# A two-block transformer kernel on one core: first gate block read early, tile order in the first block, and the last expert tiles by token half

## The chip, the core and the metric

The kernel runs on one core of a Trainium2 chip. The core has a matrix engine (TensorE, PE in the profile), a vector engine (VectorE, DVE), a scalar engine (ScalarE, ACT), GpSimd (POOL) and a queue engine (SyncE, SP) that here issues the transfers between the device memory and the on-chip memory. Matmul results land in eight banks of an accumulation memory (PSUM). The metric is the time of one launch in device microseconds; lower is better.

## The reference, cut to what matters

One sequence of 256 tokens, 1024 wide, all in float32, goes through two models one behind the other. The first is a block with a modulated norm, an input projection to gates, queries, keys and values, a causal convolution over four tokens with silu for the recurrent heads, eight-head causal attention with rotary positions, two output projections that are weighted with sigmoid gates, and a gated feed-forward of width 2816. The second is two layers of mixer, cross attention and an expert layer. The parts that the change touches are these:

```python
z = h @ w_in + b_in                        # mq, mk, mv, mo, mi, mf, aq, ak, av, ga, gb
qk = silu(causal_dwconv([mq, mk], conv_w, conv_b))
merged = sigmoid(ga) * (ym @ p_mlstm) + sigmoid(gb) * (ya @ p_moba)
x = x + g1 * (merged @ w_out)              # g1, sh2, sc2 ... = silu(c) @ ada_w + ada_b
...
# expert layer, per token and head: the 16 best of 128 x 128 key pairs
eid = take_along_axis(cand_id, pos)        # 8 heads x 16 experts of 16384
g = softmax(top)
act = gelu(einsum('td,ted->te', x, u[eid]))
x = x + einsum('te,ted->td', g * act, v[eid])
...
return rms_norm(x, final_norm)
```

## The kernel before

**Dense experts.** The expert layer (`peer`) doesn't gather. It multiplies all 16384 experts: 128 tiles of u (each 128 experts wide, 24 matmuls of 256 tokens, made by `lin_t`), a gelu, a product with a dense matrix of gates, and 128 tiles of v (12 matmuls of 512 columns, `v_tile`). A matmul in full precision is made of three: weights and activations are split into a high and a low part (`split`: a cast on ACT at L335, a difference on DVE at L336), and high x high, high x low and low x high are accumulated.

**Gates.** The dense gate matrix is built in 16 chunks of 16 tokens (L1448): DVE makes one-hot matrices from the expert numbers, PE multiplies them, ACT writes the results into a staging tile `gstg` (L1465), and SP stores the chunk to device memory (`gate_dram`, L1467). Between the steps `fill` runs u tiles. Later `load` (L1475) reads blocks of 8 expert tiles back (`gt`, L1478), one per 8 value tiles, the first when value tile 0 begins. After the chunks four more u tiles run (UX), then value tiles and the remaining u tiles alternate (L1507). The u results of blocks 7 to 9 go to device memory (`act_dram`, L1397) and come back later.

**Value tiles.** `v_tile` multiplies one row of gates with the u result (L1493), splits it and the v weights, and adds into four PSUM banks y, one for each half of the tokens (tb) and of the columns (hf): 12 matmuls at L1500. After tile 127 in layer 0, y is copied (L1525), transposed on PE (L1531), added to x (L1533), squared and scaled chunk by chunk for the next norm. In layer 1 `final` adds y to the transposed x (L1625), squares with a row sum on ACT (L1627), takes the power on POOL, multiplies with the norm's weight row and the row factor in one DVE instruction (L1633) and stores (L1634).

**First block.** Projections of `w_in_t` (37 tiles of 128 columns, `lin_t`) and of `w_in_n` (row-major, `lin_n`, evacuated at L734) are cut into steps. Tiles 0 to 8 and four steps of `w_in_n` run first; the rest is a filler (`both`, L759) that the attention (`moba`) and the recurrence (`mlstm`) call between their own instructions: 8 tiles whose evacuation is the convolution (`conv`, L697 to L702: ACT, three DVE products, ACT, one DVE product), four steps of `w_in_n`, then 4 tiles of `smo` and 16 of `sg`, which ACT evacuates alone (L729, L731). Every third step also runs one step of `ada` (L590): a 1 MB load and two reductions on DVE (L598) that make two columns of modulation. Ten of its twelve steps run there and the last two in the w_out product (L796).

**What sets the order.** Each engine and each queue executes in order. The framework places the instructions on the queues ahead of the run, by the order of the program as priority and by its own times for when operands and buffers are free, so on one queue a later instruction of the program can stand before an earlier one. On-chip buffers come from classes by size (L286): twelve of the largest size, 2064 words a partition, hold u results, gate blocks, staging tiles and split activations; three raw weight buffers of two tiles each and three pairs of split weights serve all weight streams.

## Time and profile before

| | |
|---|---|
| median of three runs | 2528.02 us (2525.88 to 2528.76) |
| the profiled execution's own time | 2529.0 us |
| its span, first to last instruction | 2527.3 us |
| PE busy | 2481.3 us, 98% of the span |
| DVE busy | 1887.2 us, 75% |
| ACT busy | 1293.1 us, 51% |
| POOL busy | 94.5 us, 4% |
| bytes moved | 536.20 MB, mean 212 GB/s |
| mean granted TensorE clock | 0.996 of full |

Busy time is the time in which an engine has at least one instruction under way; PE's matmuls are pipelined, so a busy PE is not PE at its peak. A granted clock of 1.00 is 2.4 GHz, 0.50 is 1.2 GHz.

### The profile page before, as it was taken

The page shows a single profiled execution, that of the slowest core. Times are in us where ns is not written, and L with a number is a line of the kernel's source. Part 1 is how long each engine was busy: PE and PEld are TensorE (multiplying, and loading weights), DVE is VectorE, ACT ScalarE, POOL GpSimd, SP SyncE. Part 2 cuts the span into 40 slices and gives each one's busy share as a digit, 9 for nine tenths or more (in the row PEclk, how much of TensorE's full clock was granted, in tenths as well). Part 3 has the DMA queues.
Part 4 walks back from the last instruction along what each step waited for, and adds up shares of the span by engine and source line. Part 5 has one row for each costly group of instructions (what it writes and reads, how often), then busy time and mean ns, then how long its engine had stood idle before and what let it go on. Part 6 is the DMA issues. An engine that isn't in the chain of part 4 may idle for free.

```text
span 2527.3 us, 44009 instructions
## 1 busy us (share of the span) xinstructions
PE 2481.3 (98%) x17668; PEld 2297.1 (91%) x17668; DVE 1887.2 (75%) x3438; ACT 1293.1 (51%) x2102; POOL 94.5 (4%) x107
## 2 busy tenths in 40 slices
PE   8999999999999999999999999999999999999998
PEld 6879999999999999999888889899999989998887
DVE  7887876686898976555777798767999755556776
ACT  3554555455455555444444563645455544444544
POOL 1000100221000000000000100110000000000000
PEclk9999999999999999999999999999999999999999
DMA  8556565554555796567875544345457866579753
GB/s 336 183 181 229 204 230 205 184 169 150 173 175 199 273 313 221 194 222 241 296 257 193 191 172 150 117 150 167 168 192 270 312 221 212 202 241 298 277 187 130
DMA packets 197468, 536.20 MB, mean 212 GB/s; under 512 B 9232, under 2 KB 82192, under 8 KB 191760
## 3 DMA queue, kind: packets, MB, share of 16 engines
q1 hardware_dynamic: 197264, 533.40, 61.2%
q8 instruction: 138, 2.26, 0.4%
q14 instruction: 66, 0.54, 0.1%
HBM read 492.47 MB, written 40.89 MB: 211 GB/s over the span
## 4 chain that ended last, share of the span: by engine, by line
PE 82%; DVE 8%; issue 6%; DMA 2%; ACT 1%; POOL 0%; SPq 0%; DVEq 0%; POOLq 0%; ACTq 0%
PE mm L1500 23%; PE mm L400 9%; PE mm L401 9%; PE mm L402 9%; PE sm L400 8%; PE sm L401 8%; PE sm L402 8%; DVE wL L336 2%; PE sm L1462 1%; PE sm L1463 1%; PE mm L431 1%; PE mm L432 1%; PE mm L430 1%; DMA gt<-gate_dram 1%; DMA raw<-in_wk 1%
## 5 line engine op out<-in xcount | busy, mean ns | idle before, releaser
L335 ACT CAST wH<-raw 128x1024 fp32r<-128x1024 f32 x789 | 826.6, 1049 | 992.4 <-PE sm L401 312.9
L336 DVE TENSOR_TENSOR wL<-raw,wH 128x1024 fp32r<-128x1024 f32 x789 | 966.8, 1226 | 455.4 <-ACT wH L335 449.8
L400 PE MATMUL sm<-uH,wH 128*128 128x256 f32 x2048 | 584.3, 285 | 2.1 <-ACT wH L335 2.0
L402 PE MATMUL sm<-uH,wL 128*128 128x256 f32 x2048 | 577.3, 282 | 3.8 <-DVE wL L336 3.8
L401 PE MATMUL sm<-uL,wH 128*128 128x256 f32 x2048 | 578.6, 283 | 0.0
L400 PE MATMUL mm<-nH,wH 128*128 128x256 f32 (+1 forms) x1432 | 410.6, 288 | 4.6 <-ACT qraw L726 2.4
L401 PE MATMUL mm<-nL,wH 128*128 128x256 f32 (+1 forms) x1432 | 404.8, 283 | 1.2 <-DVE nL L616 1.0
L402 PE MATMUL mm<-nH,wL 128*128 128x256 f32 (+1 forms) x1432 | 403.6, 283 | 0.8 <-DVE wL L336 0.6
L400 PEld LDWEIGHTS sm<-uH,wH 128*128 128x128 f32 x2048 | 386.3, 189 | 6.6 <-ACT wH L335 2.5
L402 PEld LDWEIGHTS sm<-uH,wL 128*128 128x128 f32 x2048 | 386.0, 189 | 5.6 <-DVE wL L336 5.6
L401 PEld LDWEIGHTS sm<-uL,wH 128*128 128x128 f32 x2048 | 386.7, 189 | 3.6
L1500 PE MATMUL mm<-wH,pwh 128*128 128x512 f32 x1024 | 317.6, 391 | 4.0 <-ACT pwh L335 4.0
L1500 PE MATMUL mm<-wL,pwh 128*128 128x512 f32 x1024 | 316.8, 391 | 0.0
L1500 PE MATMUL mm<-wH,pwl 128*128 128x512 f32 x1024 | 316.3, 390 | 0.0
L400 PEld LDWEIGHTS mm<-nH,wH 128*128 128x128 f32 x1432 | 270.1, 189 | 9.8 <-issue 3.5
L401 PEld LDWEIGHTS mm<-nL,wH 128*128 128x128 f32 x1432 | 270.9, 189 | 2.1 <-DVE nL L616 1.2
L402 PEld LDWEIGHTS mm<-nH,wL 128*128 128x128 f32 x1432 | 270.2, 189 | 2.5 <-DVE wL L336 1.4
L1500 PEld LDWEIGHTS mm<-wL,pwh 128*128 128x128 f32 x1024 | 192.8, 188 | 41.2
L1500 PEld LDWEIGHTS mm<-wH,pwl 128*128 128x128 f32 x1024 | 192.5, 188 | 41.0
L1500 PEld LDWEIGHTS mm<-wH,pwh 128*128 128x128 f32 x1024 | 185.8, 188 | 37.3 <-ACT pwh L335 4.4
L1493 DVE TENSOR_TENSOR pw<-act,gt 128x256 f32<-128x256 f32 x256 | 108.6, 424 | 19.9 <-DMA gt<-gate_dram 12.6
L336 DVE TENSOR_TENSOR pwl<-pw,pwh 128x256 fp32r<-128x256 f32 x256 | 108.8, 425 | 12.6 <-ACT pwh L335 6.6
(452 smaller groups left out, 3085.6 us busy)
## 6 DMA issues: line engine op xcount, KB each, us to landing
raw<-in_u SPq DMA_DIRECT2D x128, 1024.0 KB, 5.0
raw<-in_v SPq DMA_DIRECT2D x128, 1024.0 KB, 5.0
gate_dram<-gstg SPq DMA_DIRECT2D x32, 1024.0 KB, 4.8
gt<-gate_dram SPq DMA_DIRECT2D x32, 1024.0 KB, 8.3
raw<-in_ada SPq DMA_DIRECT2D x24, 1024.0 KB, 4.9
raw<-in_w_gu SPq DMA_DIRECT2D x22, 1024.0 KB, 4.9
raw<-in_w_in_t SPq DMA_DIRECT2D x18, 1024.0 KB, 5.1
raw<-in_pq SPq DMA_DIRECT2D x16, 1024.0 KB, 5.0
```

The source lines that it names most:

```text
L335: self.nc.scalar.copy(H, src)
L336: self.nc.vector.tensor_sub(L, src, H.bitcast(F32))
L400: mm(ps[:, :w], H[:, o:o + P], xH[:, c], start=c == 0, stop=False)
L401: mm(ps[:, :w], H[:, o:o + P], xL[:, c], start=False, stop=False)
L402: mm(ps[:, :w], L[:, o:o + P], xH[:, c], start=False, stop=c == kc - 1)
L430: mm(pss[tb], xh, H[:, o:o + 512], start=c == 0, stop=False)
L431: mm(pss[tb], xl, H[:, o:o + 512], start=False, stop=False)
L432: mm(pss[tb], xh, L[:, o:o + 512], start=False, stop=c == kc - 1)
L1462: nc.tensor.matmul(ps[:, k * P:k * P + P], at(ah), at(o1), start=True, stop=False)
L1463: nc.tensor.matmul(ps[:, k * P:k * P + P], at(al), at(o1), start=False, stop=True)
L1493: nc.vector.tensor_mul(w.rearrange("p (c t) -> p c t", c=16), act[b][:, j].rearrange("p (c t) -> p c t", c=16), box[b][:, :, j])
L1500: nc.tensor.matmul(y[tb * 2 + hf], a[:, sl], m[:, hf * 512:hf * 512 + 512], start=n == 0 and a is wh and m is vH, stop=n == P - 1 and a is wl)
```

## The change

It has five parts. The weight columns of `w_in_t` are reordered so that the eight convolution tiles and the first eight gate tiles alternate, and the filler takes sixteen tiles before it turns to `w_in_n`; the evacuation follows the new numbering. The last two steps of `ada` run after tile 3 of p_moba and tile 3 of w_out, in place of tiles 2 and 5 of w_out. In the expert layer the first gate block gets its tile `gfirst` before the chunks; chunks 0 to 13 are loaded into it from device memory after chunk 13 is stored, and the parts of chunks 14 and 15 are copied by ACT out of the staging tile. The matmuls of the last three value tiles are held back and made at tile 127, token half 0 first, then token half 1 by column half; the copies behind them in layer 0 follow that order. In `final`, x is multiplied with the norm's weight row ahead of the power, and the product with the row factor is made by ACT for one column half and by DVE for the other.

```diff
 RB = 7
 SB = 3
-VL, RI, MD, UX, M1, M2, D1, D2, AS, AW, PQ0, NQ0, FT, F0, FH, FS, FL, FO = 6, 5, 1, 4, 1.25, 1.5, 0.5, 0.75, 3, 3, 13, 3, 0.6, 1, 0.5, 1, 4, 1.075
+VL, RI, MD, UX, M1, M2, D1, D2, AS, PQ0, NQ0, FT, F0, FH, FS, FL, FO = 6, 5, 1, 4, 1.25, 1.5, 0.5, 0.75, 3, 13, 3, 0.6, 1, 0.5, 1, 4, 1.075
 REPL = -3e38
 GSCALE = 16384.0
...
     A["positions"] = np.ascontiguousarray(i["positions"])
     A["final_row"] = np.ascontiguousarray(i["final_norm_2"].reshape(1, D))
     A["ada"] = _pack_rows(i["ada_w"][0])
-    A["w_in_t"] = _pack_t(np.concatenate([gate, w_in[:, 2056:3080], w_in[:, 0:1024], w_in[:, 1536:2048], w_in[:, 3592:5640]], axis=1))
+    A["w_in_t"] = _pack_t(np.concatenate([gate, w_in[:, 2056:3080], *(w for j in range(8) for w in (w_in[:, j * P:j * P + P], w_in[:, 3592 + j * P:3720 + j * P])), w_in[:, 1536:2048], w_in[:, 4616:5640]], axis=1))
     A["w_in_n"] = _pack_n(np.concatenate([w_in[:, 3080:3592], w_in[:, 1024:1536]], axis=1))
     A["b_nat"] = np.ascontiguousarray(np.concatenate([b_in[3080:3592], b_in[1024:1536]])[None])
     A["p_mlstm"] = _pack_t(i["p_mlstm"][0])
...
                 turn.append((e - 1, raw))
                 if e > 1:
                     rope(*turn.pop(0))
-            elif e < 17:
+            elif e < 25 and e % 2:
+                c = (e - 9) // 2
                 raw = self.t(None, "qraw", [P, T])
-                nc.scalar.activation(raw, ps, AF.Identity, bias=self.vec("b_qk", e - 9))
-                conv(e - 9, raw)
-            elif e < 21:
-                nc.scalar.activation(smo[:, e - 17], ps, AF.Tanh, scale=0.5, bias=hb[:, e - 17:e - 16])
+                nc.scalar.activation(raw, ps, AF.Identity, bias=self.vec("b_qk", c))
+                conv(c, raw)
+            elif 24 < e < 29:
+                nc.scalar.activation(smo[:, e - 25], ps, AF.Tanh, scale=0.5, bias=hb[:, e - 25:e - 24])
             else:
-                nc.scalar.activation(sg[:, e - 21], ps, AF.Tanh, scale=0.5, bias=hb[:, e - 17:e - 16])
+                c = (e - 10) // 2 if e < 25 else e - 21
+                nc.scalar.activation(sg[:, c], ps, AF.Tanh, scale=0.5, bias=hb[:, 4 + c:5 + c])
         def evac_n(g, tb, ps):
             nc.vector.tensor_add(vnat[:, g, tb], ps, b_nat[:, g * 512:g * 512 + 512])
...
         next(mg)
         def rest():
-            for _ in range(8):
+            for _ in range(16):
                 yield next(zt)
             yield from zn
             yield from zt
...
             nc.vector.tensor_add(m, a, merged[:, e])
             self.split(mH[:, e], mL[:, e], m)
+        moved = []
         for g in (self.lin_t("p_moba", 8, 4, (ya[:, :4], ya[:, 4:]), ev_ma), self.lin_t("p_mlstm", 8, 4, (ym[:, :4], ym[:, 4:]), ev_mm)):
-            self.run(g)
+            for i, _ in enumerate(g):
+                if i == 3 and not moved:
+                    moved.append(next(ada, None))
         nc.vector.tensor_scalar(self.mod[:, 16:24], self.mod[:, 16:24], 0.5, None, op0=ALU.mult)
         geff = self.t(None, "geff", [P, 8])
         nc.vector.scalar_tensor_tensor(out=geff, in0=self.mod[:, 32:40], scalar=1.0, in1=self.vecn("norm2", 0, 8), op0=ALU.add, op1=ALU.mult)
         n2 = Norm(self, geff)
         n2.shift = self.mod[:, 24:32]
         for i, _ in enumerate(self.lin_t("w_out", 8, 8, (mH, mL), self.residual(n2, lambda e: self.mod[:, 16 + e:17 + e]))):
-            if i % AW == AW - 1:
+            if i == 3:
                 next(ada, None)
         self.run(ada)
         self.tap("xa", self.x)
...
             nc.vector.tensor_scalar(ghlT[:, sl, 0], gT, GSCALE, None, op0=ALU.mult)
             nc.vector.scalar_tensor_tensor(out=ghlT[:, sl, 1], in0=gT, scalar=GSCALE, in1=ghlT[:, sl, 0], op0=ALU.mult, op1=ALU.subtract)
         gd = self.dram.tile([16, P, P * 16], F32, name=f"gate_dram{l}")
+        gfirst = self.t(None, "gt", [P, 16, P])
         for ch in range(16):
             stg = self.t(None, "gstg", [P, P, 16])
             for sub in range(2):
...
                     nc.scalar.activation(dst, ps.rearrange("p (t i) -> p i t", t=4), AF.Copy, scale=1.0 / GSCALE)
                 self.fill(FO)
             nc.sync.dma_start(gd[ch], stg.rearrange("p i t -> p (i t)"))
+            i0 = 8 * order[0]
+            if ch == 13:
+                nc.sync.dma_start(gfirst[:, :14], gd[:14, :, i0 * 16:i0 * 16 + P].rearrange("c p f -> p c f"))
+            elif ch > 13:
+                nc.scalar.copy(gfirst[:, ch], stg[:, i0:i0 + 8].rearrange("p i t -> p (i t)"))
         self.drain()
         for _ in range(UX):
             next(u_gen)
...
         def load(n):
             b = order[n]
-            gt = self.t(None, "gt", [P, 16, P])
-            nc.sync.dma_start(gt, gd[:, :, b * P:b * P + P].rearrange("c p f -> p c f"))
+            gt = self.t(None, "gt", [P, 16, P]) if n else gfirst
+            if n:
+                nc.sync.dma_start(gt, gd[:, :, b * P:b * P + P].rearrange("c p f -> p c f"))
             box[b] = gt.rearrange("p c (i t) -> p c i t", i=8)
             if RB <= b < RB + SB:
                 act[b] = self.t(None, "act", [P, 8, T])
                 nc.sync.dma_start(act[b].rearrange("p i t -> p (i t)"), sd[b - RB])
+        rest = []
         def v_tile(n):
             if n == 0:
...
             nc.vector.tensor_mul(w.rearrange("p (c t) -> p c t", c=16), act[b][:, j].rearrange("p (c t) -> p c t", c=16), box[b][:, :, j])
             self.split(wh, wl, w)
             vH, vL = next(vst)
-            for tb in range(2):
-                sl = slice(tb * P, tb * P + P)
-                for a, m in ((wh, vH), (wh, vL), (wl, vH)):
-                    for hf in range(2):
-                        nc.tensor.matmul(y[tb * 2 + hf], a[:, sl], m[:, hf * 512:hf * 512 + 512], start=n == 0 and a is wh and m is vH, stop=n == P - 1 and a is wl)
+            rest.append([(hf, a, m, n == 0 and a is wh and m is vH, n == P - 1 and a is wl) for a, m in ((wh, vH), (wh, vL), (wl, vH)) for hf in range(2)])
+            if n < P - 3:
+                products(0)
+                products(1)
+                rest.clear()
+            elif n == P - 1:
+                products(0)
+                for p in rest:
+                    p.sort(key=lambda q: q[0])
+                products(1)
+        def products(tb):
+            for hf, a, m, first, last in chain(*rest):
+                nc.tensor.matmul(y[tb * 2 + hf], a[:, tb * P:tb * P + P], m[:, hf * 512:hf * 512 + 512], start=first, stop=last)
         if l == 1:
...
         out = Norm(self, self.vecn("mix_norm", 8, 8))
         out.late = out.fast = True
         ys = []
-        for g in range(2):
-            for tb in range(2):
+        for tb in range(2):
+            for g in range(2):
                 yt = self.t(None, "py", [P, 512])
-                (nc.scalar.copy if tb else nc.vector.tensor_copy)(yt, y[tb * 2 + g])
+                (nc.scalar.copy if g else nc.vector.tensor_copy)(yt, y[tb * 2 + g])
                 ys.append(yt)
         for g in range(2):
             for tb in range(2):
                 ps = self.sm()
                 for c in range(4):
-                    nc.tensor.transpose(ps[:, c * P:c * P + P], ys[g * 2 + tb][:, c * P:c * P + P], self.ident)
+                    nc.tensor.transpose(ps[:, c * P:c * P + P], ys[tb * 2 + g][:, c * P:c * P + P], self.ident)
                 xs = self.x[:, 4 * g:4 * g + 4, tb * P:tb * P + P]
                 nc.vector.tensor_add(xs, xs, ps.rearrange("p (c t) -> p c t", c=4))
             for c in range(4):
...
                 nc.vector.tensor_add(xs, xs, y[tb * 2 + hf])
                 junk = self.t(None, "fj", [P, 512])
                 nc.scalar.activation(junk, xs, AF.Square, accum_out=ss[:, hf:hf + 1])
+            xf = [self.t(None, "fx", [P, 512]) for _ in range(2)]
+            for hf in range(2):
+                nc.vector.tensor_mul(xf[hf], xn[:, tb, hf * 512:hf * 512 + 512], frow[:, hf * 512:hf * 512 + 512])
             nc.vector.tensor_add(ss[:, :1], ss[:, :1], ss[:, 1:])
             r = self.pow_col(ss[:, :1], 1.0 / D, EPS, 1)
             for hf in range(2):
                 sl = slice(hf * 512, hf * 512 + 512)
                 o = self.t(None, "fo", [P, 512])
-                nc.vector.scalar_tensor_tensor(out=o, in0=xn[:, tb, sl], scalar=r, in1=frow[:, sl], op0=ALU.mult, op1=ALU.mult)
+                if hf:
+                    nc.vector.tensor_scalar(o, xf[hf], r, None, op0=ALU.mult)
+                else:
+                    nc.scalar.activation(o, xf[hf], AF.Copy, scale=r)
                 nc.sync.dma_start(self.out[0, tb * P:tb * P + P, sl], o)
     def build(self):
```

## Rows read from the trace of the kernel before

**Rows 1.** The page, its first part: busy us, share of span, instructions.

```profile
PE 2481.3 (98%) x17668; PEld 2297.1 (91%) x17668; DVE 1887.2 (75%) x3438; ACT 1293.1 (51%) x2102; POOL 94.5 (4%) x107
```

**Rows 2.** Windows: stretch, length, then each engine's busy us; clock, DMA share, GB/s.

```profile
118.00:200.00 82.00, 76.29 (x488) 63.40 (x487) 73.21 (x192) 46.29 (x103) 4.98 (x8) 0.96 0.50 180
146.00:156.00 10.00, 9.85 (x29) 6.47 (x30) 7.12 (x18) 5.17 (x13) 1.41 (x2) 0.66 0.18 74
250.00:300.00 50.00, 47.93 (x398) 47.20 (x397) 46.86 (x82) 25.59 (x42) 6.13 (x6) 1.00 0.62 214
```

**Rows 3.** Timeline of PE, the stage with the convolution: start, length, idle before.

```profile
141.59 0.39 PE L400 MATMUL mm<-nH,wH 128*128 128x256 f32 x1 [2.38 <-ACT qraw L726]
```

**Rows 4.** Single lines of code on DVE: shortest, median and longest ns.

```profile
L699 DVE SCALAR_TENSOR_TENSOR qk<-qraw,vecs,qk x24: 347/476/676, 126.0 to 173.9; 128x255 f32<-128x255 f32 x8, 128x254 f32<-128x254 f32 x8, 128x253 f32<-128x253 f32 x8
L702 DVE SCALAR_TENSOR_TENSOR qk<-ra,qk x8: 405/426/685, 131.1 to 175.0; 128x256 f32<-128x256 f32 x8
L598 DVE CUSTOM_DVE_ANT_0 adaj<-raw,cb x48: 1199/1218/1753, 21.5 to 379.5; 128x1024 bf16<-128x1024 f32 x48
```

**Rows 5.** Timeline of SP's queue around the first layer's last gate chunks.

```profile
916.45 1.03 SPq L1467 DMA_DIRECT2D gate_dram<-gstg  x1
...
931.83 0.33 SPq L1467 DMA_DIRECT2D gate_dram<-gstg  x1
...
938.49 0.37 SPq L1478 DMA_DIRECT2D gt<-gate_dram  x1
940.56 3.35 SPq L1397 DMA_DIRECT2D act_dram<-sact  x2
```

**Rows 6.** Timeline of PE before the first value matmul, both expert layers.

```profile
946.11 0.39 PE L400 MATMUL sm<-uH,wH 128*128 128x256 f32 x1 [1.02 <-ACT wH L335]
...
947.96 0.72 PE L1500 MATMUL mm<-wH,pwh 128*128 128x512 f32 x2 [1.35 <-ACT pwh L335]
...
2028.16 0.39 PE L400 MATMUL sm<-uH,wH 128*128 128x256 f32 x1 [1.02 <-ACT wH L335]
...
2031.32 1.02 PE L1500 MATMUL mm<-wH,pwh 128*128 128x512 f32 x2 [2.65 <-ACT pwh L335]
```

**Rows 7.** Windows: last gate chunks of layer 0, first value tiles of layer 1.

```profile
900.00:941.00 41.00, 41.00 (x406) 40.67 (x404) 28.96 (x25) 23.56 (x40) 0.00 (x0) 1.00 0.92 319
2031.00:2035.00 4.00, 3.68 (x9) 2.91 (x10) 3.06 (x7) 1.35 (x4) 0.00 (x0) 0.57 0.67 198
```

**Rows 8.** An ACT copy of 128x128, shortest, median and longest ns.

```profile
L504 ACT COPY pT<-sm x16: 254/272/307, 128.2 to 1620.4; 128x128 f32<-128x128 f32 x16
```

**Rows 9.** Timeline of PE behind the value tiles of layer 0.

```profile
1436.21 0.62 PE L400 MATMUL mm<-nH,wH 128*128 128x256 f32 x3 [0.91 <-ACT nH L236]
```

**Rows 10.** Chain of waits, value matmuls before the end: start, us, count.

```profile
2298.87 198.59 PE mm L1500 x876
```

**Rows 11.** Timeline of the last microseconds.

```profile
2510.40 1.23 DVE L336 TENSOR_TENSOR wL<-raw,wH 128x1024 fp32r<-128x1024 f32 x1 [1.49 <-ACT wH L335]
...
2517.75 0.61 PE L1500 MATMUL mm<-wH,pwl 128*128 128x512 f32 x2
...
2518.25 1.28 DVE L1625 TENSOR_TENSOR xn<-xn,mm 128x512 f32<-128x512 f32 x2 [0.16 <-ACT fj L1627]
...
2520.12 0.18 ACT L1627 ACTIVATION_READ_ACCUMULATOR fj<-xn 128x1 f32 x1
...
2521.78 0.15 DVE L1628 TENSOR_TENSOR fss<-fss 128x1 f32<-128x1 f32 x1
...
2522.80 1.41 DVE L1633 SCALAR_TENSOR_TENSOR fo<-xn,pr,frow 128x512 f32<-128x512 f32 x2 [0.67 <-POOL pr L473]
```

**Rows 12.** Store of the output: KB, us to landing; 128x512 copies of ACT.

```profile
out<-fo SPq DMA_DIRECT2D x4, 256.0 KB, 2.0
...
L1525 ACT COPY py<-mm x2: 586/589/592, 1432.9 to 1433.3; 128x512 f32<-128x512 f32 x2
```

**Rows 13.** Timeline of ACT, first staging writes of layer 0's last chunk.

```profile
926.92 1.08 ACT L1465 ACTIVATE gstg<-sm 128x512 f32<-128x512 f32 x2
```

## The prediction, made before the result was known

> **What bounds the kernel now.** I read the page's engine table first: TensorE (PE) is busy for 98% of the span, VectorE (DVE) for 75% [rows 1]. So the kernel is a long PE stream, and a change that removes no matmul can only win back PE idle time (2527.3 - 2481.3 = 46.0 us), half-clock time, and the tail behind the last matmul. I then cut the span into stages at the places that the diff touches.
>
> Stage one is the part of the first block in which projections, convolution and block attention run together, 118 to 200 us. In its 82 us PE is busy 76.3, so idle 5.7, while DVE is busy 73.2; around 146 to 156 us the granted clock averages 0.66 [rows 2]. With levels of 1.0 and 0.5 that is 10 x (1 - 0.66) / 0.5 = 6.8 us at half clock, which costs 3.4 us of matmul work. The longest single gap, 2.38 us, ends on ACT's copy of a convolution tile out of PSUM (L726) [rows 3]: the evacuation was late, not the weights. What the gaps and the slow clock hold together is 5.7 + 3.4 = 9.1 us.
>
> Stage two is the p_moba, p_mlstm and w_out products, 250 to 300 us: PE idle 2.1 us, DVE busy 46.9 of 50 [rows 2].
>
> Stage three is the hand-over from building the gates to the value products, once in each expert layer. The store of the last gate chunk is issued at 931.83 and the load of the first gate block only at 938.49, when that store has landed (6.7 us); PE runs out of work twice before the first value matmul at 947.96 [rows 5, 6]. The gaps are 1.02 + 1.35 = 2.4 us in layer 0 and 1.02 + 2.65 = 3.7 us in layer 1 [rows 6]. In layer 0 the clock stayed at full level; in layer 1 it averages 0.57 over the 4 us that follow [rows 7], 3.4 us at half clock, 1.7 us lost. Together 2.4 + 3.7 + 1.7 = 7.8 us.
>
> The last is the two ends of the expert layers. At the end of layer 0 PE waits 0.91 us for the first normalized chunk [rows 9]. At the very end the last matmuls finish at 2517.75 + 0.61 = 2518.36 [rows 11], so 8.9 us of the span lie behind them.
>
> **First block: order of the tiles.** Matmuls, evacuations and vector instructions stay as many; 8 gate tiles now stand between the 8 convolution tiles. One convolution costs DVE three products of 0.48 and one of 0.43, 1.86 us, eight of them 14.9 us [rows 4]. Before, they come in eight successive filler steps; now they are spread over sixteen, and the two groups of row-major products (L734 evacuates them) come behind them. The upper bound is all of the 9.1 us, the lower bound nothing, since DVE's work is the same. DVE gives the estimate: it is busy 73.2 of 82 us, so the stage can't shrink by more than 8.8 even with DVE at 100%. I take half of 9.1: **4.5 us**.
>
> **First block: modulation rows.** The last two of the twelve steps (each two reductions of 1.22 us on DVE [rows 4] and a 1 MB load) move from tiles 2 and 5 of w_out to tile 3 of p_moba and tile 3 of w_out. Nothing is removed, so at best the 2.1 us of idle PE go; at worst the 2.4 us of reductions make p_moba's weight splits late instead. DVE has only 3.1 us free in these 50, so I take less than half: **0.9 us**. The extra load passes SP ahead of p_mlstm's and w_out's weights; I cost that at nothing, as DVE is the full engine there and the weights stand in SP ahead of their use, and keep the loss of 2.4 as bound.
>
> **Gate hand-over.** The load of chunks 0 to 13 can go when chunk 13's store has landed: 916.45 + 6.7 = 923.1 on the old clock. It then needs some 8.5 us (from the issue at 938.49 to the first matmul at 947.96 is 9.5, of which the product and the cast take about one), so it is there at about 931.6, when chunk 15 is just being stored. Chunks 14 and 15 come by two copies on ACT of 128x128, 0.27 us each [rows 8], four in both layers, 1.1 us; they hide behind matmuls, since PE is busy for all of 900 to 941 us while ACT is busy 23.6 of 41 [rows 7]; uncovered they would cost that 1.1 us. PE comes free at 946.11 - 1.02 = 945.1 [rows 6], some 12 us after the operands. What remains are transitions; I take **7.0 us** of the 7.8, between bounds of 0 (below) and 7.8.
>
> **Last expert tiles by token half.** The 36 matmuls of the last three tiles stay. A matmul of this shape takes 198.59 / 876 = 0.227 us of the stream [rows 10], so token half 0 is now complete 18 x 0.227 = 4.1 us before the end, and the first column half of token half 1 2.0 us before it. PE now needs tile 127's operands early: it starts the 36 at about 2518.4 - 36 x 0.227 = 2510.2 (some 0.3 sooner with the four transposes that stood between them) and comes to tile 127 after 12, at about 2512.6. The last of that tile's weight splits was done at 2510.40 + 1.23 = 2511.6 [rows 11]. So no stall is my value; the margin of 1 us is thin, and 1.4 us (half 0 of a tile late by its own length) goes into the bound below. In layer 0 three of four copies out of PSUM now lie under matmuls; the additions and squares behind the transposes stay on the path. Of the 0.9 us gap there I take **0.5**, bounds 0 and 0.9.
>
> In layer 1 I rebuild the tail. Before: DVE's two additions for token half 1 end at 2518.25 + 1.28 = 2519.53, ACT has squared and summed at 2520.12 + 0.18 = 2520.30, but DVE joins the two sums only at 2521.78, because the output products of half 0 keep it busy; half 1's products run from 2522.80 to 2524.2, and the last store lands 2.0 after that [rows 11, 12]. Now half 0 is out of the way. After the last matmul: 0.1 and one addition, 0.64; ACT's square to the end of its accumulator, 2520.30 - 2519.53 = 0.8; joining, scaling and power to the start of the product, 2522.80 - 2521.78 = 1.0; one product, 0.71; a second store issue behind the first, 0.4 (SP's issues take 0.33 to 0.37 [rows 5]); landing 2.0; the 1.1 us that the span runs on (2527.3 - 2526.2). That is 6.8 against 8.9: **2.1 us**. The half of the product that goes to ACT costs no more than its 128x512 copies, 0.59 [rows 12]; the four added products with the norm row, 0.71 each on DVE like the products they precede, run while ACT squares; if none of that cover held it would cost 1.4. Bounds -0.7 (that, and the 1.4 above) and 3 (the four additions of half 0 and their squares are wholly gone from the tail).
>
> The Trainium skill ("VectorE: DVE Perf Modes", section "The perf-mode tier table") lets a tensor-by-scalar product in fp32 from SBUF run twice as fast as a product of two tensors. By it the last product on DVE would be about 0.3 us shorter and the sum 0.3 us larger; no row here has this shape, and the sum above doesn't use it.
>
> **Sum.** 4.5 + 0.9 + 7.0 + 0.5 + 2.1 = 15.0 us off the profiled execution's 2529.0, 2514.0. That execution is 1.0 above the median 2528.02, so against the median I forecast **2513**.
>
> **Rivals.**
> *One: the alternation gives nothing.* For it: DVE, not PE, is the fullest engine of stage one for long stretches, and no DVE instruction goes. Against it: the 2.38 us gap sits on a convolution evacuation. Time: 2513 + 4.5 = 2517.5.
> *Two: the hand-over still waits.* SP waits for chunk 13's store before it can issue the load; if the load stands directly behind that store, SP is held 6.3 us, and weight loads behind it are late while the DMA engines are already 92% busy [rows 7]. The wait on the gate block becomes one on weights. Against it: before, the load was issued just as the store landed, and two activation stores that the program has ahead of it were issued after it, from 940.56 [rows 5]; the order of SP is planned by time, not by program. Time: 2513 + 7.0 = 2520. The Trainium skill ("DMA: Bandwidth & Descriptors", "Anatomy of one DMA — SWDGE (gpsimd) path") says that a semaphore wait happens on the issuing sequencer, before dispatch; this speaks for this rival, and the trace agrees only so far that SP is in order.
> *One and two together:* 2524.5, within the bound of no change.
> *Three: slower, by buffers.* The early gate tile takes one of the 12 slots of its size. Two slots hold the split activations and seven the u results, so three were left for staging, two now. A chunk's first write to staging comes 4.9 us before its store (926.92 to 931.83) and stores come 7.7 apart [rows 5, 13]: with two slots it comes 15.4 - 4.9 = 10.5 us after the store that frees the slot, which lands in 6.7; no wait. Should another tile of that size be alive and only one slot be left, it comes 7.7 - 4.9 = 2.8 after, and each chunk is 6.7 - 2.8 = 3.9 us late. For some 12 chunks a layer that is 94 us: about 2607. It decides from five late chunks on (20 us against the 15). Against it: the count above.
>
> **How the numbers follow.** What counts as a change for this kernel is 0.2%, 5 us. Forecast 0.52 (its own range 2508 to 2517, from the halves that I took); rival one 0.20; two 0.12; both 0.09; three 0.07. Leaving out three and both together (0.16) and a few hundredths at the low end, where every term is near its bound (9.1 + 2.1 + 7.8 + 0.9 + 3 = 22.9 would be 2505), the range is 2506 to 2523. Faster: 0.52 + 0.20 + 0.12 less 0.05 for cases one and two that end above 2523, 0.79; same 0.09 + 0.05 = 0.14; slower 0.07.
>
> **What would show it.** In the profile after: no gap before the first value matmul in either layer and no half clock behind it (hand-over right); the load of the first gate block issued about 15 us before the first value matmul; the gap on L726's convolution copy gone and PE idle below 3 us between 118 and 200 (alternation right); DVE idle near zero there with the stage still 82 us long (rival one); PE waiting for a weight split between chunks 13 and 15 (rival two); ACT's staging writes waiting for stores, chunks over 8 us apart (rival three); last matmul to end of span 6.8 us. A wrong count of what DVE can still take in stage one would make the forecast wrong soonest.

## The result, and the profile after

The changed kernel takes 2512.63 us in the median of five runs (2510.81 to 2513.2), against 2528.02 before: ratio 0.9937, 95% interval 0.9926 to 0.9947. Its profiled execution took 2513.2 us with a span of 2511.5, 15.8 less than before. The forecast was 2513. All times here are medians of fast runs; one of the twelve runs of undo_handover below, 2682.23 us, was slow and is left out.

The engine table of the page, against [rows 1]: PE has lost 6.7 us of busy time (part of it half-clock time) and 9.1 of idle.

```profile
PE 2474.6 (99%) x17668; PEld 2293.0 (91%) x17668; DVE 1885.4 (75%) x3440; ACT 1294.5 (52%) x2108; POOL 97.8 (4%) x107
```

Where the 15.8 lie, from instructions that both timelines have, as the change of each distance (times in the span before and after in brackets): up to the first weight gap of the first block (71.93 before, 72.93 after) +1.0, within the start's own variation (71.1 to 73.0 in all runs); to the end of the recurrence (244.39, 240.88) -4.5; to the row sums behind w_out (299.30, 294.54) -1.25; to layer 0's gates (781.30, 776.71) +0.2; to the last value matmul of layer 0 (1433.04, 1426.63) -1.8; to the first mixer matmul (1436.21, 1430.09) +0.3; to layer 1's gates (1861.11, 1854.07) -0.9, in stages that the change doesn't touch; to the last value matmul (2518.36, 2504.37) -6.95; to the end of the span -1.8.

The windows of the changed kernel answer to [rows 2]; columns as there.

```profile
118.00:200.00 82.00, 80.10 (x524) 68.17 (x524) 74.25 (x195) 46.99 (x107) 8.35 (x8) 0.96 0.54 191
154.00:158.00 4.00, 2.71 (x14) 2.15 (x15) 3.90 (x15) 3.01 (x9) 0.00 (x0) 0.81 0.68 258
158.00:162.00 4.00, 4.00 (x14) 2.70 (x14) 4.00 (x6) 0.47 (x2) 2.81 (x2) 0.50 0.42 108
162.00:166.00 4.00, 4.00 (x31) 4.00 (x31) 2.91 (x7) 1.58 (x3) 0.00 (x0) 0.84 0.78 258
250.00:300.00 50.00, 48.94 (x409) 48.21 (x408) 44.67 (x75) 26.49 (x42) 7.00 (x7) 1.00 0.63 212
```

Stage one has 1.9 us of PE idle left of 5.7, and the gap of [rows 3] is gone. But the stretch at 0.50 (1.2 of 2.4 GHz) is not: (0.19 + 0.50 + 0.16) x 4 / 0.5 = 6.8 us, as long as before, now behind two short gaps:

```profile
154.66 0.38 PE L400 MATMUL mm<-nH,wH 128*128 128x256 f32 x1 [0.81 <-ACT wH L335]
...
156.12 0.43 PE L512 MATMUL sm<-pT,vnat 128*64 128x128 f32 x2 [0.63 <-ACT pT L504]
...
918.79 0.22 PE L1469 MATMUL sm<-oo,oa 128*128 128x128 f16 x1 [0.82 <-ACT sact L1401]
...
940.16 0.72 PE L1525 MATMUL mm<-wH,pwh 128*128 128x512 f32 x2
```

The last row is the first value matmul, with no gap in front, against [rows 6]; layer 1 has none either and keeps full clock. The row above it is new: a gap of 0.82 among the last gate chunks, one in each layer. The timelines of ACT and SP show what is late there. Chunk 14's staging writes come at 918.64, all four at once, 7.7 behind chunk 13's second pair, where chunk 13's two pairs are 3.8 apart:

```profile
907.13 1.08 ACT L1472 ACTIVATE gstg<-sm 128x512 f32<-128x512 f32 x2
910.95 1.08 ACT L1472 ACTIVATE gstg<-sm 128x512 f32<-128x512 f32 x2
918.64 2.05 ACT L1472 ACTIVATE gstg<-sm 128x512 f32<-128x512 f32 x4
920.72 0.30 ACT L1479 COPY gt<-gstg 128x128 f32<-128x128 f32 x1
```

```profile
912.05 0.80 SPq L1474 DMA_DIRECT2D gate_dram<-gstg  x1
...
918.54 0.37 SPq L1477 DMA_DIRECT2D gt<-gate_dram  x1
...
920.72 1.21 SPq L1474 DMA_DIRECT2D gate_dram<-gstg  x1
...
928.51 0.32 SPq L1474 DMA_DIRECT2D gate_dram<-gstg  x1
```

The early load goes out 6.5 us behind chunk 13's store and 21.6 ahead of the first value matmul. At the end of layer 0, against [rows 9], the gap in front of the mixer has grown to 1.64: a weight split now stands between the copies out of PSUM and the additions. The first rows are DVE's before the change, where the last split starts 1.6 us ahead of the end of the value matmuls (1433.04). The rows after the change follow; there it starts 0.15 behind that end (1426.63).

```profile
1431.45 1.23 DVE L336 TENSOR_TENSOR wL<-raw,wH 128x1024 fp32r<-128x1024 f32 x1 [1.50 <-ACT wH L335]
1432.60 1.28 DVE L1525 COPY py<-mm 128x512 f32<-128x512 f32 x2
```

```profile
1426.17 0.68 DVE L1550 COPY py<-mm 128x512 f32<-128x512 f32 x1
...
1426.78 1.21 DVE L336 TENSOR_TENSOR wL<-raw,wH 128x1024 fp32r<-128x1024 f32 x1
...
1427.91 2.47 DVE L1558 TENSOR_TENSOR x_res<-x_res,sm 128x512 f32<-128x512 f32 x4
...
1430.09 0.62 PE L400 MATMUL mm<-nH,wH 128*128 128x256 f32 x3 [1.64 <-ACT nH L236]
```

The tail, against [rows 11], is 2511.5 - 2504.37 = 7.13 us. Both sums are there at 2505.96, but the join starts at 2506.31, behind the two products with the norm row:

```profile
2503.91 1.28 DVE L1650 TENSOR_TENSOR xn<-xn,mm 128x512 f32<-128x512 f32 x2
...
2505.10 1.28 DVE L1655 TENSOR_TENSOR fx<-xn,frow 128x512 f32<-128x512 f32 x2
...
2505.77 0.19 ACT L1652 ACTIVATION_READ_ACCUMULATOR fj<-xn 128x1 f32 x1
2506.31 0.15 DVE L1656 TENSOR_TENSOR fss<-fss 128x1 f32<-128x1 f32 x1
...
2507.31 0.72 ACT L1664 ACTIVATE fo<-fx,pr 128x512 f32<-128x512 f32 x1 [1.35 <-POOL pr L473]
2507.31 0.49 DVE L1662 TENSOR_SCALAR fo<-fx,pr 128x512 f32<-128x512 f32 x1 [0.67 <-POOL pr L473]
```

The product by one scalar takes 0.49 here, a product of two tensors 0.64. The Trainium skill ("VectorE: DVE Perf Modes", "The perf-mode tier table") gives the first twice the rate, for operands of 2048 elements; the trace, with 512, agrees in the direction, not in the size.

### The profile page after: what moved, and what is told of

Read it like the earlier page. It is cut to its first block, busy times and chain, and to the rows that moved or that the text cites. A ratio compares the mean times of both kernels' runs of the same rounds, so it can differ in the third digit from the quotient of the medians.

```text
span 2511.5 us, 44019 instructions
## 1 busy us (share of the span) xinstructions
PE 2474.6 (99%) x17668; PEld 2293.0 (91%) x17668; DVE 1885.4 (75%) x3440; ACT 1294.5 (52%) x2108; POOL 97.8 (4%) x107
## 3 DMA queue, kind: packets, MB, share of 16 engines
q8 instruction: 138, 2.26, 0.4%
## 4 chain that ended last, share of the span: by engine, by line
PE 84%; DVE 7%; issue 6%; DMA 1%; ACT 1%; POOL 0%; SPq 0%; POOLq 0%; DVEq 0%; ACTq 0%
PE mm L1525 23%; PE mm L400 9%; PE mm L402 9%; PE mm L401 9%; PE sm L400 8%; PE sm L401 8%; PE sm L402 8%; DVE wL L336 2%; PE sm L1469 1%; PE sm L1470 1%; PE mm L432 1%; DMA raw<-in_ada 1%; PE mm L430 1%; PE mm L431 1%; PE sm L1011 1%
```

## The experiments

All are edits of the changed kernel, timed against the kernel before on the same chip. They were timed in three sessions, in which the kernel before took 2528.2, 2529.8 and 2528.9 us, so 1 or 2 us between two kernels of different sessions say little by themselves; there the distances in the traces decide. "Stage one" below is the distance from the first block-attention matmul (125.14 in the changed kernel) to the end of the recurrence (240.88): 115.7 after, 120.2 before.

**The order of the first block's tiles, undone** (undo_tile_order).

```
-            elif e < 25 and e % 2:
+            elif e < 17:
...
-            for _ in range(16):
+            for _ in range(8):
```

> The changed kernel with only the order of the first block's tiles put back (eight convolution tiles in a row). Theory: the alternation is worth the 4.5 us by which the shift of the first block's landmarks grew over that stage in the changed kernel (from +1.0 at 72 us to -3.5 at the end of the recurrence), all of it from shorter gaps, since the half-clock stretch only moved (6.8 us at half clock before and after). Time 2517.1 (2512.6 + 4.5); the 2.4 us gap before L400 that ends on the convolution's copy returns near 141 us, and PE idle in 118 to 200 us is about 5.7 again instead of 1.9. Rival (the alternation gives nothing, and the first block is shorter through the moved modulation steps or by chance): 2512.6 to 2514, idle in 118 to 200 stays near 1.9.

Measured: 2513.92, ratio 0.9944 (0.9931 to 0.9957), 1.3 above the changed kernel and not to be told from it. The gap is back, PE idle is 82 - 77.3 = 4.7, and stage one takes 117.5:

```profile
140.95 0.38 PE L400 MATMUL mm<-nH,wH 128*128 128x256 f32 x1 [2.34 <-ACT qraw L726]
```

So neither theory holds as written. The gaps are the alternation's, as the first says; the time follows only in part, for two reasons that lie in the clock. The half-clock stretch of stage one is 3.4 us here and 6.8 in the changed kernel. It differs between kernels whose first block is the same: 3.4 us in undo_handover, 10.2 in gate_tile_in_quarters; with one profiled execution of each, whether the kernel or the execution decides is open. And at the end of layer 0, which the edit doesn't touch, the clock falls to half for 3.4 us behind a gap as long as the changed kernel's, and the mixer's first part takes 1.4 us longer (9.5 instead of 8.1). PE's timeline and windows of this run, then the same window of the changed kernel:

```profile
1430.61 0.62 PE L400 MATMUL mm<-nH,wH 128*128 128x256 f32 x3 [1.65 <-ACT nH L236]
1430.00:1436.00 6.00, 5.26 (x29) 5.06 (x30) 6.00 (x17) 5.51 (x16) 0.00 (x0) 0.72 0.63 257
1430.00:1436.00 6.00, 5.79 (x47) 5.59 (x47) 5.90 (x16) 5.00 (x15) 0.00 (x0) 1.00 0.58 236
```

What the alternation takes away in stage one is best read where the stretches are equally long: 2.6 us with 3.4 at half clock (117.5 here, 114.9 in undo_handover) and 4.5 us with 6.8 (120.2 before, 115.7 after). Without the cost of the stretch, taken as half its length, stage one takes 115.8 here and 116.8 before in the old order, and 111.9 to 113.2 in nine kernels with the new.

**The gate hand-over, undone** (undo_handover).

```
-            if ch == 13:
-                nc.sync.dma_start(gfirst[:, :14], ...)
-            elif ch > 13:
-                nc.scalar.copy(gfirst[:, ch], ...)
...
-            gt = self.t(None, "gt", [P, 16, P]) if n else gfirst
+            gt = self.t(None, "gt", [P, 16, P])
```

> The changed kernel with the gate block of the first eight value tiles loaded after the last chunk again, no early tile and no copies. Theory: the hand-over is worth what the landmarks moved across it, 1.8 us in layer 0 and 6.9 us in layer 1, 8.7 in all, which is already net of a new 0.82 us gap per layer in front of chunk 14: time 2521.3; gaps before the first value matmul of 1.0 + 1.4 us in layer 0 and 1.0 + 2.7 us in layer 1, with a half-clock stretch of some 3.4 us behind the second; both 0.82 us gaps gone. Rival (part of layer 1's 6.9 us belongs to a clock stretch that comes and goes by itself, or to drift elsewhere): 2517 to 2519, layer 1's gap back but no half clock behind it.

Measured: 2523.2 in the median of eleven runs (2517.7 to 2526.8), ratio 0.998 (0.9972 to 0.9989), so some 10.6 slower, more than the theory. Between the landmarks layer 0 loses 2.9 and layer 1 7.8. The gaps come back, and at both the clock falls (PE's timeline, then windows):

```profile
940.43 1.22 PE L1518 MATMUL mm<-wH,pwh 128*128 128x512 f32 x2 [1.65 <-ACT pwh L335]
2026.09 1.22 PE L1518 MATMUL mm<-wH,pwh 128*128 128x512 f32 x2 [2.26 <-ACT pwh L335]
2024.00:2034.00 10.00, 7.91 (x22) 6.27 (x23) 5.06 (x10) 2.85 (x6) 0.00 (x0) 0.66 0.96 304
940.00:946.00 6.00, 5.57 (x18) 4.51 (x19) 3.34 (x8) 2.63 (x6) 0.00 (x0) 0.72 0.79 301
```

That is 6.8 and 3.4 us at half clock, where the kernel before had 3.4 and none. Gaps of 1.02 + 1.65 and 1.02 + 2.26, and 5.1 for the clock, make 11.0; the two gaps of 0.82 that are gone give some 2.5 back (next run). Some 2 us are left, and the trace shows two things outside that sum: at the end of layer 0 the clock is at half for 3.4 us, as in undo_tile_order, some 1.5 us; and in layer 1 five groups of eight value tiles take 44.80 us each instead of 44.53, 1.35 together. Why this pace differs is open: it is 44.80 in the kernel before too, and 44.37 in undo_tile_order, which has the hand-over of the changed kernel.

**The new gap of 0.82** (gate_tile_in_quarters, thirteen_slots).

```
-        gfirst = self.t(None, "gt", [P, 16, P])
+        gfirst = [self.t(None, "gt4", [P, 4, P]) for _ in range(4)]
...
-            if ch == 13:
-                nc.sync.dma_start(gfirst[:, :14], ...)
+            for k, c0, c1 in {5: [(0, 0, 4)], 9: [(1, 4, 8)], 13: [(2, 8, 12), (3, 12, 14)]}.get(ch, ()):
+                nc.sync.dma_start(gfirst[k][:, :c1 - c0], gd[c0:c1, ...])
```

> The changed kernel with the early gate tile held in four tiles of a smaller buffer class (four chunks each), so that it takes no slot of the staging tiles' ring; three of the four loads go out earlier, and the product of the first eight value tiles is cut in four. Theory (the early gate tile holds up chunk 14's staging tile through the ring of buffers): the 0.82 us gap near 918.8 and 1997.9 us goes in both layers, chunk 14 is stored 7.7 us behind chunk 13 instead of 8.7; 24 more products on DVE per layer hide. Time 2512.6 - 1.6 = 2511.0. Rival (the gap comes from SP's queue being held by the wait for chunk 13's store, whatever the tile): the gap stays or moves to other chunks, 2512.6 or more.

Measured: 2508.59, ratio 0.9919 (0.9906 to 0.9932), 4.0 below the changed kernel. Both gaps are gone and chunk 14 is stored 7.7 behind chunk 13, although SP holds the load as long as before (6.4 us behind the store; its queue):

```profile
911.48 0.32 SPq L1474 DMA_DIRECT2D gate_dram<-gstg  x1
917.90 0.37 SPq L1477 DMA_DIRECT2D gt<-gate_dram  x1
919.18 0.33 SPq L1474 DMA_DIRECT2D gate_dram<-gstg  x1
```

So SP's wait is not the cause. The gain is 4.0 and not 1.6: from the gates to the first value matmul each layer is 1.25 shorter, and layer 1's groups of eight tiles take 44.4 us, five of them some 0.8 us less together. That second part need not be the edit's, since undo_tile_order has it with the old gate tile. The edit does three things at once (another class, earlier and smaller loads, a product in four parts), and no run takes them apart.

```
-    CLASSES = ((32, 14), (128, 8), (256, 14), (512, 8), (1024, 4), (2064, 12))
+    CLASSES = ((32, 13), (128, 8), (256, 14), (512, 4), (1024, 4), (2064, 13))
```

> The changed kernel with thirteen buffers of the largest class instead of twelve (four of the 512-element class given up for it), the early gate tile as changed. It asks why chunk 14's staging writes come late in the changed kernel (at 918.64, right behind the issue of the early load at 918.54, instead of 7.7 us behind chunk 13's at 914.8). Theory one (slots: two staging slots are too few): with a thirteenth slot chunk 14 is on time and the 0.82 us gap goes. Theory two (order: buffers of one class are handed out in the order of the program, so chunk 14's tile gets its slot only when the early gate tile ahead of it has had its first write, which is the load that waits for chunk 13's store): the gap of 0.82 stays in both layers, though a slot is free. One look; time as the changed kernel, or a few us more where the smaller class runs short.

Measured: 2528.75 in a single run. Some 16 us are lost elsewhere, far more than foreseen (8 us in layer 0's value tiles, 8.8 in layer 1's); that the smaller classes cost them (one buffer of the smallest went too) is not shown. The gap of 0.83 stays in both layers. ACT's timeline:

```profile
909.19 1.08 ACT L1472 ACTIVATE gstg<-sm 128x512 f32<-128x512 f32 x2
912.73 0.38 ACT L1401 ACTIVATE sact<-sm 128x256 f32<-128x256 f32 x1
916.54 0.38 ACT L1401 ACTIVATE sact<-sm 128x256 f32<-128x256 f32 x1
916.82 2.05 ACT L1472 ACTIVATE gstg<-sm 128x512 f32<-128x512 f32 x4
```

The load went out at 917.07, behind these writes, so in this run they did not wait for it: they stand late in ACT's order itself, behind the activation at 916.54. A further slot doesn't help, the quarters in another class do; that speaks for theory two, the order in which the program is laid out around the shared ring. That the planner does it this way is inferred from the two kernels, not seen.

**The token halves and the last product** (three runs).

```
-            if n < P - 3:
+            if n < P - 3 or l == 0:
```

> The changed kernel with the last three value tiles of layer 0 in their old order (each tile's matmuls together) and the old order of the copies there; layer 1 as changed. Theory (in layer 0 the token-half order loses 0.3 us, because the mixer's first weight splits now stand between the copies and the additions): from the last value matmul of layer 0 to the first matmul of the mixer 3.1 to 3.2 us instead of 3.46, gap in front of it 0.9 instead of 1.64; time 2512.3, which is too little for the clock on the wall to tell. Rival (the order is worth 0.5 us in layer 0, as the forecast had it, and something else took 0.8): the distance grows to 3.9 or more, time 2513.1.

Measured: 2512.82, ratio 0.9935 (0.9922 to 0.9948), no difference in time to the changed kernel. In the timeline the distance is 1429.82 - 1426.65 = 3.17 and the gap 0.92; the theory holds, the order loses 0.3 in layer 0. It can lose more: of the seven kernels with the long gap (1.62 to 1.65) in front of the mixer two show the half-clock stretch behind it that costs some 1.5 us, of the seven with the short one (0.91 to 0.92) none. For both layers undone the line is `if n < P:`.

> The changed kernel with the last three value tiles of both layers in their old order, the last product split over ACT and DVE as changed. Theory: undoing the split of the product alone took the tail from 7.13 to 7.78 us, so of the 1.8 us that the tail won the token-half order has the other 1.2: tail 8.3, layer 0's end 0.27 shorter; time 2512.6 + 1.2 - 0.3 = 2513.5. Rival (with the old order the four norm-row products stand among four additions behind the last matmul, 4 x 0.64): tail 9.0 or more, as long as before the change; time 2514.2 or more. Rival (the token-half order is nothing by itself): tail 7.1.

Measured: 2516.36, ratio 0.995 (0.9938 to 0.9962), 3.7 above the changed kernel. The tail is 2514.4 - 2504.09 = 10.3 us, longer than before the change: the rival's size. Half 0's norm-row products now run ahead of half 1's second addition, and half 1's own come after it, all four behind the last matmul:

```profile
2504.57 1.29 DVE L1654 TENSOR_TENSOR fx<-xn,frow 128x512 f32<-128x512 f32 x2
...
2505.84 0.68 DVE L1649 TENSOR_TENSOR xn<-xn,mm 128x512 f32<-128x512 f32 x1
...
2507.65 1.29 DVE L1654 TENSOR_TENSOR fx<-xn,frow 128x512 f32<-128x512 f32 x2
```

```
-                if hf:
-                    nc.vector.tensor_scalar(o, xf[hf], r, None, op0=ALU.mult)
-                else:
-                    nc.scalar.activation(o, xf[hf], AF.Copy, scale=r)
+                nc.vector.scalar_tensor_tensor(out=o, in0=xn[:, tb, sl], scalar=r, in1=frow[:, sl], ...)
```

> The changed kernel with only the last product of the output put back: both halves on DVE as one product of three operands, no products with the norm row ahead of it. Theory: in the changed kernel the two norm-row products of 0.64 each stand between the last addition and the join of the two sums and hold it up by 0.35 us (the accumulators end at 2505.96, the join starts at 2506.31), while the split of the last product over ACT and DVE saves one product of 0.71 in a row: undone, the tail is 0.35 us longer, 7.5 instead of 7.13, time 2513.0. The join then starts within 0.1 us of the second accumulator. Rival (the split of the product was worth the whole gain of the tail): 8.5 or more. Rival (the late join eats it all): 7.1.

Measured: 2513.75, ratio 0.9938 (0.9924 to 0.9951); tail 2510.9 - 2503.12 = 7.78, join 0.03 behind the second sum. The theory's direction, 0.65 where it said 0.35; the time, 1.1 above the changed kernel in another session, can't be told from it.

**The modulation move, undone** (undo_modulation_move).

```
-                if i == 3 and not moved:
-                    moved.append(next(ada, None))
...
-            if i == 3:
+            if i % 3 == 2:
```

> The changed kernel with the last two modulation steps back at tiles 2 and 5 of w_out. Theory: from the end of the recurrence to the first matmul of the row broadcast behind w_out 54.9 us instead of 53.7 to 53.9 (the 1.1 us by which the landmarks moved), the gap of 1.64 us that ends on DVE's weight split in w_out is back; time 2513.7. Rival (the stage is DVE's, and what is won there is lost in front of p_moba): distance as in the changed kernel, 2512.6.

Measured: 2514.24, ratio 0.994 (0.9927 to 0.9954); from 239.91 to 294.83, 54.9 us, and the w_out gap is back at 1.73. The theory holds: 1.26 us against the changed kernel's 53.7, 0.9 to 1.5 against the eight other kernels with this stage as changed (53.5 to 54.0).

```profile
286.29 0.39 PE L402 MATMUL mm<-mH,wL 128*128 128x256 f32 x1 [1.73 <-DVE wL L336]
```

**Together, and the half clock** (four runs). The combined kernel has the quarters, the token halves in layer 1 only, and DVE's half of the last product in one instruction.

> The changed kernel with three edits: the early gate tile in quarters (2508.6 when run alone), the token-half order in layer 1 only (0.27 us shorter at layer 0's end in the profile), and in the last product DVE's half as one product of three operands, so that only one norm-row product stands ahead of the join. Theory: the three add up, the join starts within 0.1 us of the second accumulator and the tail is 0.3 us shorter than 7.13; time 2508.6 - 0.3 - 0.3 = 2508.0. Rival (DVE's longer product, 0.71 in place of 0.49, is last and eats the earlier join): tail 7.1, time 2508.3.

Measured: 2508.56, ratio 0.9915 (0.9901 to 0.9928); distance in front of the mixer 3.17, join 0.03 behind the second sum, tail 6.97. DVE's longer product gives half of the earlier join back; the sum is that of the quarters alone.

```
-AS = 3
+AS = 4
```

> The combined kernel with a modulation step at every fourth filler tile of the first block instead of every third, so that DVE's pairs of reductions of 1.2 us fall at other places. It tells what brings the half-clock stretch (3.4 to 10.2 us long so far, always behind 140 to 156 us). Theory: the stretch comes behind short gaps of PE among the small matmuls of the block attention, and these follow DVE's reductions; moved, the gaps near 154.7 and 156.1 us change and the stretch begins elsewhere or is gone: up to 3 us faster than the combined kernel, 2505 to 2508. Rival (the clock falls there whatever the gaps): the same stretch of 3.4 to 10.2 us at 152 to 166 us, same time; later steps are crowded, so up to 1 us slower.

Measured: 2508.51, ratio 0.9919 (0.9905 to 0.9932), no change from combined. Stage one has no gap in 118 to 200 us and no half clock and is 5.5 us shorter, more than the theory said; the time is the rival's, because the steps left over come in front of the next norm, with 4.24 us of idle and 6.8 at half clock that begin in it (timeline):

```profile
288.92 0.58 PE L400 MATMUL mm<-nH,wH 128*128 128x258 f32 x1 [4.24 <-ACT nH L246]
```

So the slow stretch followed the gaps, and the steps' places make them: the nine kernels with the two short gaps at 153 to 156 us all have a stretch, of 3.4 to 10.2 us.

```
-                if i % AS == AS - 1:
+                if i in (3, 7, 11, 15, 17, 19, 21, 23, 25, 27):
```

> The combined kernel with the modulation steps of the first block at filler tiles 3, 7, 11, 15 and then at every second one to 27, ten of them as before: the small matmuls of the block attention keep the wide spacing that took away every gap and the half clock in the run with every fourth tile, and the steps are all done in time, so that the 4.24 us wait for the norm behind w_out, which that run bought, is gone. Theory: PE busy for all of 118 to 200 us at clock 1.00, end of the recurrence at about 237.2 instead of 239.3, no gap over 2 us near 289, no half clock in the first block: 2508.5 less 2.1 to 3 = 2505.5 to 2506.5. Rival (six steps close together crowd DVE between 200 and 250 us, where weight splits come late): stage one as said, but the gain is given back before 300 us: 2508.5.

Measured: 2502.8, ratio 0.99 (0.9886 to 0.9915), 5.8 below combined and 9.8 below the changed kernel: the fastest here, and below the theory's 2505.5 to 2506.5. Combined was timed in another session, but the traces agree: the span is 5.7 us shorter, 4.8 of it in stage one, which ends at 234.6 and not at the theory's 237.2, and 1.0 in p_moba to w_out. PE is busy 81.7 of 82 at full clock:

```profile
118.00:200.00 82.00, 81.66 (x568) 70.89 (x567) 76.11 (x197) 50.48 (x112) 8.56 (x8) 1.00 0.57 200
250.00:300.00 50.00, 49.57 (x413) 49.03 (x412) 44.30 (x75) 29.23 (x49) 6.99 (x7) 1.00 0.59 206
```

> The kernel combined_steps_spread with only the order of the first block's tiles put back to eight convolution tiles in a row. It measures the alternation without the half-clock stretch that came and went in the other comparison (3.4 us of it with the old order, 6.8 and 10.2 with the new). Theory (the alternation takes 3.5 us of gaps away): 3.5 us slower than combined_steps_spread, plus 1.7 or 3.4 where its gaps bring a half-clock stretch: 2509 to 2512.5; gap of 2.3 us behind the convolution's copy near 141 us. Rival (the modulation steps made the gaps, and the order of the tiles is nothing once they are spread): the same time within 1 us, no gap at 141.

Measured: 2512.93, ratio 0.9942 (0.9929 to 0.9954), 10.1 slower than with the alternation, in the same session. Its edit is that of undo_tile_order. The windows show PE idle of 5.5 us and some 3.4 at half clock, and the recurrence then waits 2.41 for POOL:

```profile
118.00:200.00 82.00, 76.53 (x513) 65.08 (x513) 72.25 (x190) 47.74 (x108) 6.62 (x8) 0.98 0.53 191
...
246.33 0.43 PE L460 MATMUL sm<-ident,mF 128*128 128x128 f32 x2 [2.41 <-POOL mF L937]
```

From the first block-attention matmul to the row sums behind w_out the two profiled executions are 8.8 us apart: 10.2 longer in stage one (6.8 of it idle PE, 1.7 half-clock time, most of the rest matmuls that the other kernel makes behind it), 1.4 shorter behind it. The start differs by 1.6 more, as it does between other runs. The theory's range is just missed, and its gap of 2.3 us comes as several of 1.1, 0.7, 1.7 and 1.2; the rival is refuted.

## Why the prediction was right, and where it was not

The total came within 1 us, partly by luck. The five terms came to 16.0 us in the landmarks instead of 15.0, off both ways; a later start took 1.0 of them back, and 0.7 more came from stages that the change doesn't touch.

- **Order of the tiles, 4.5.** The landmarks moved by 4.5, but not by the forecast's sum. "Half of 9.1" took gaps and slow clock alike; 3.8 of 5.7 us of gaps went and none of the 3.4 for the clock. The 3.4 itself is high: with the same gaps, 3.4 us more at half clock make stage one 1.3 longer (115.7 after, 117.1 in gate_tile_in_quarters), so 6.8 us cost some 2.6. Undone alone the alternation shows as 1.3 in time, rival one's size, and as 2.6 where the stretches are equal; with the steps spread it shows as 10.1, or 8.8 in the first block. The limit from DVE was not what decided: in the best kernel PE is the full engine (81.7 of 82) and DVE is at 76.1. That the modulation steps decide how much of the alternation is seen was missed.
- **Modulation rows, 0.9.** Measured 1.25 from the landmarks and 0.9 to 1.5 undone.
- **Gate hand-over, 7.0.** The largest miss in size: 8.75 by the landmarks, above the bound of 7.8, and 10.6 undone. The bound counted gaps and clock of one execution; it left out the pace of layer 1's value tiles (five groups of eight, 44.80 before and 44.53 after, 1.35 us, cause open), and undone, the clock fell at both gaps. The wait of SP, rival two, cost nothing: other issues stood between store and load, and SP was held for 2.2 us and not 6.3. The Trainium skill ("DMA: Bandwidth & Descriptors", "Anatomy of one DMA — SWDGE (gpsimd) path") has the wait on the issuing sequencer; the trace agrees, SP issues nothing from 916.3 to 918.5, but the store behind it went out only 0.2 us later behind its activation than its neighbours did.
- **Rival three** came true on a small scale, not by the mechanism that it named: one chunk per layer was late, a gap of 0.82 each. One slot more left the gap as it was; that the writes' place in ACT's order decides is inferred.
- **Layer 0's end, 0.5.** Wrong in sign: 0.3 lost. The step said that three copies lie under matmuls; it left out DVE's weight splits, which now come just then, 1.6 us ahead of the last value matmul's end and 0.15 behind it. That the three held-back tiles keep the three pairs of buffers for split weights until the end is a reading of the program that would give this; no run tests it.
- **The tail, 2.1.** Measured 1.8. The chain was as worked out, except that the norm-row products do not fully run while ACT squares: the join is 0.35 late. ACT's half of the last product took 0.72 and not 0.59. The forecast's price for no cover at all, 1.4, equals what undo_token_half lost against the kernel before (10.3 against 8.9), but not by the same sum: there all four products, 2.6 us, stand behind the last matmul, and the split of the last product gives part of it back.

## What to carry to other kernels

Moving work off a full engine's crowded stretch pays together with the other work placed there: reordering tiles was worth some 2.6 to 4.5 us beside one placement of the modulation steps and some 9 beside another, so try such placements jointly and judge each by its stage. Read a stage together with its half-clock time before putting a difference of 1 to 3 us down to an edit. When a tile is given a longer life, look at where its neighbours in the same ring of buffers stand in their engine's order, not only at whether a slot is free. When matmuls are held back to the end, ask which buffers they keep and what of the next stage will start behind them.

## What the runs showed of the hardware

The half-clock stretches in these profiles, those at the very end left out, were 3.4, 6.8 or 10.2 us long. In stage one of the changed kernel the clock fell behind gaps of only 0.81 and 0.63 us, 1.46 apart, among small matmuls of the block attention; in layer 0 of the kernel before it stayed up behind gaps of 1.02 and 1.35 [rows 6], and in undo_handover it fell in the second of two gaps of 1.02 and 1.65 at the same place. In front of layer 0's mixer a gap of 1.62 to 1.65 stands ahead of the same matmuls in seven kernels; the clock fell behind it for 3.4 us in undo_tile_order and undo_handover and stayed up in the other five. So one gap alone does not tell what the clock does.
